# A hybrid encoder layer in split fp32: where the stationary matmul operands lie in SBUF

## The chip, the core and the metric

One core of one Trainium2 chip runs the whole program, in one launch. The metric is the device time of that launch in microseconds, as the median of three runs. Beside it stands one profiled execution, from which all rows of the profile come.

## What is computed

The reference is one inference step of one layer for 256 prompt tokens and 128 sample tokens (8 streams of 16), 384 in all, with a model width of 2048. In short:

```
u = rmsnorm(x);  P = u @ w_in          # columns: pool | z | x,B,C | dt | gates
A = causal pooling means of P.pool, mapped per group by pool_w, scaled
B = Mamba-2 scan of (conv(x,B,C), dt) + D skip, gated by silu(z), group-normed
m = sigmoid(g_A) * (A @ w_pool_proj) + sigmoid(g_B) * (B @ w_ssd_proj)
x += rmsnorm(m @ w_out)
x += rmsnorm(relu(rmsnorm(x) @ w_up)^2 @ w_down)
```

All in fp32. Outputs are x and the new pooling, convolution and scan states of both groups.

## The kernel before

**Split matmuls.** A large matrix product is made of three TensorE (PE) matmuls in the type fp32r, which takes fewer bits of a number than fp32. Each operand is split into a high part (a copy rounded to fp32r) and a low part (the rest); the product is high by high, high by low and low by high (`mm3`, L79 to L82). A matmul has a stationary operand, 128 rows by 128 columns, which is loaded first (a LDWEIGHTS row in the profile, engine PEld), and a moving operand, whose columns then stream through.

**Weights stationary.** In `proj` (L93) the weights are the stationary operand and the 384 tokens the moving one. `wfetch` (L61) loads a unit of 128 x 1024 numbers, eight tiles of 128 x 128, through the queue of SP; `wsplit` (L66) makes the high part `wh` on ScalarE (ACT, L71) and the low part `wl` on VectorE (DVE, L73); `half` (L84) issues the 24 matmuls of the unit. The pool `wpool` holds three buffers each of `w`, `wh` and `wl`. All projections by w_in (129 column tiles of two units each), w_pool_proj and w_up (two units a tile), w_ssd_proj (four) and the maps by pool_w (`pool_map`) go this way. The matmuls' names in the profile begin with `pj_`, or are `pw`.

**Activations stationary.** In `moving` (L639) it is the other way round: the weights of w_out and w_down stream as 512 columns, and tokens are the stationary operand: `mh`, `ml` for w_out (names `wo`, lines L646 to L648) and `hh`, `hl` for w_down (`wd`, the same lines).

**Stages.** First loads, the pooling columns and their maps (to 382 us about), gates and w_pool_proj (to 457 us), then for each of eight groups the conv, z and scan (to 1390 us), then w_ssd_proj (`pj_sp`, to 1656 us), w_out (to 1791 us), and the MLP in eight rounds of `pj_up` and `wd` (to 2860 us), with the last norm at the end. The scan's own matmuls (L434 to L584) are small; all but `su` (L584, stationary `bst`, moving `xst`, 256 columns, fp32r) are plain fp32, which PE takes in two records each, or transposes. Which instruction goes when on an engine is planned by the framework from the program's order and dependences; tiles get their addresses from pools, which are stacks at the left and the right end of SBUF, in steps of 32 bytes.

**Addresses.** The program's allocation gives each tile an address in the partition. Every slice of 128 columns is 512 bytes, so that a tile's place past a line of 128 bytes is also that of each of its slices. In bytes past such a line:

| operand | role | pool | place before | place after |
|---|---|---|---|---|
| wh, wl (all pj_ and pw) | stationary | wpool | 64 | 0 |
| hh, hl (wd) | stationary | phg2 | 64 | 0 |
| mh, ml (wo) | stationary | mp | 96 | 0 |
| bst (su) | stationary | phd1 | 96 | 0 |
| xs, xdw, xdt, yis, Cm, ssum, x1 (scan, transposes, norms) | stationary | phd, pha, res | 64 | 0 |
| ones (bc) | stationary | consts | 0 | 0 |
| cum, dt, dtw, nb (11 transposes, L347) | stationary | phc | 32 | 96 |
| xgh, xgl (pj_x, z, p, ga, gb, dt) | moving | xgp | 96 | 0 |
| ah, al (pj_pp) | moving | phc | 0 | 64 |
| dh, dl (pw) | moving | phc2 | 96 | 32 |
| abh, abl (pj_sp); x1h, x1l (pj_up) | moving | phe, pga | 64 | 0 |
| wh, wl (wd, wo) | moving | wpool | 64 | 0 |
| xst (su), Bk, E, hs | moving | phd | 64 | 0 |

**Lines that the change touches.** C_END and V_END (L31, L32) are the widths of the constant tiles `cst` and `vec` (L45, L46), which lie ahead of `wpool`. `small` (L142) is the first pool on the right; `tok` (L212) lies in it. At L371 to L382 the pool `phd1` gets `cstate` with its load on GpSimd's queue (POOL), the three `cbuf` with a memset each, and the two `bst` with a memset each. `mp` (L608) holds `mh` and `ml`.

Of the kernel before, what the change touches and what calls it, by code (L numbers as in the profile page):

```python
# [6 lines left out]
F32 = mybir.dt.float32  # L7
F32R = mybir.dt.float32r
# [6 lines left out]
P = 128  # L15
# [12 lines left out]
NG = 6  # L28

C_IDENT, C_ONES, C_MASK, C_CM, C_BM = 0, 128, 256, 768, 1024  # L30
C_RC, C_SCAN, C_END = 1032, 1096, 1480  # L31
V_GPRE, V_GMLP, V_PSC, V_CW, V_CB, V_NRM, V_DSK, V_DTB, V_ALOG, V_END = 0, 16, 32, 48, 240, 288, 320, 352, 353, 354  # L32


def build(ctx, tc, io):
    nc = tc.nc
    v, s, te, gp, sy = nc.vector, nc.scalar, nc.tensor, nc.gpsimd, nc.sync
# [55 lines left out]
    def proj(units, rhs, name):  # L93
        o = mmtile(f"pj_{name}")[:, :T]
        for q, src in enumerate(units):
            half(o, q, wload(src, f"{name}_{q}"), rhs)
        return o
# [44 lines left out]
    small = main.enter_context(tc.tile_pool(name="small", bufs=1, side="right"))  # L142
# [66 lines left out]
    s.copy(rstd, rms_bc(pa, acc, DM, "x"))  # L209
    pha.close()  # L210

    tok = small.tile([P, 11, NH], F32, name="tok")  # L212
    decb = small.tile([P, NH, NB], F32, name="decb")
    with tc.tile_pool(name="phc", bufs=1, reuse_waits="tile") as pc, tc.tile_pool(name="phc2", bufs=2, reuse_waits="tile") as pc2:
# [3 lines left out]
        for i in range(2):  # L218
            b = pc.tile([P, 519], F32, name=f"pbuf{i}")
# [148 lines left out]
    with tc.tile_pool(name="phd", bufs=2, reuse_waits="tile") as pd, tc.tile_pool(  # L368
        name="phd1", bufs=1, reuse_waits="tile"
    ) as pd1:  # L370
        cst_ = pd1.tile([P, 48, 9, 3], F32, name="cstate")  # L371
        gp.dma_start(cst_, io["state_conv"])
        cbuf = []
        for i in range(3):
            b = pd1.tile([P, 24, 19], F32, name=f"cbuf{i}")
            gp.memset(b[:, 0, :3], 0.0)
            cbuf.append(b)
        bst = []
        for i in range(2):
            b = pd1.tile([P, 4, 2, P], F32R, name=f"bst{i}")  # L380
            gp.memset(b.bitcast(F32), 0.0)
            bst.append(b)  # L382
        seg = lambda a: a.rearrange("p (b t) -> p b t", b=24)
        ncv = [0]

# [222 lines left out]
    mp = mpool.enter_context(tc.tile_pool(name="mp", bufs=1, side="right", reuse_waits="tile"))  # L608
    ms_ = []
    with tc.tile_pool(name="phe", bufs=1, reuse_waits="tile") as pe1, tc.tile_pool(name="phe2", bufs=3, reuse_waits="tile") as pe2:  # L610
        ab = []
        for i in range(32):
            a = pe2.tile([P, T], F32, tag="ar", name=f"ar{i}")
            sy.dma_start(a, a_scr[i])
            h = pe1.tile([P, T], F32R, name=f"abh{i}")
            l = pe1.tile([P, T], F32R, name=f"abl{i}")
            s.activation(h, a, AF.Copy)
            v.tensor_tensor(l, a, h.bitcast(F32), ALU.subtract)
            ab.append((h, l))
        for n in range(KD):  # L620
            ma = pe2.tile([P, T], F32, tag="mar", name=f"mar{n}", bufs=2)
            gb = pe2.tile([P, T], F32, tag="gbr", name=f"gbr{n}", bufs=2)
            sy.dma_start(ma, ma_scr[n])
            sy.dma_start(gb, gb_scr[n])
            ps = proj([io["w_ssd"][n, q] for q in range(4)], ab, f"sp{n}")
            v.tensor_tensor(gb, ps, gb, ALU.mult)
            v.tensor_tensor(ma, ma, gb, ALU.add)
            h = mp.tile([P, T], F32R, name=f"mh{n}")
            l = mp.tile([P, T], F32R, name=f"ml{n}")
            s.activation(h, ma, AF.Copy)  # L630
            v.tensor_tensor(l, ma, h.bitcast(F32), ALU.subtract)
            ms_.append((h, l))

    res = ctx.enter_context(tc.tile_pool(name="res", bufs=1, reuse_waits="tile"))

# [45 lines left out]
    with tc.tile_pool(name="phf", bufs=1, side="right", reuse_waits="tile") as pf, tc.tile_pool(  # L681
        name="phf2", bufs=2, side="right", reuse_waits="tile"
# [45 lines left out]
    with tc.tile_pool(name="phg", bufs=1, reuse_waits="tile") as pg, tc.tile_pool(  # L728
        name="phg2", bufs=2, reuse_waits="tile"
# [18 lines left out]
        for c8 in range(NC):  # L748
            hh = []
            for f8 in range(8):  # L750
                f = c8 * 8 + f8
# [166 lines left out]
```

## Time and profile before

| | |
|---|---|
| median of three runs | 2873.96 us (2873.9 to 2875.45) |
| span of the profiled execution, first to last instruction | 2874.5 us |
| instructions in the profile | 40193, of them 16165 matmuls and 16165 weight loads |
| PE busy | 2850.2 us, 99% |
| DVE, ACT, POOL busy | 1548.4, 1106.4, 142.2 us |
| DMA | 448.79 MB, mean 156 GB/s |

The page gives no other time of the profiled execution than its span, which is 0.5 us above the median of the runs.

In rows of the timeline the columns are start in us, duration in us, engine, line, operation, tile written and tiles read, shapes, and how many were merged into the row. A matmul's duration in the profile runs on after the next one has started, so that durations of neighbours overlap. In rows of groups (line, engine, operation) the numbers behind the bar are busy us, mean ns of one, then the engine's idle time before them and what ended it. `128*128 128x384` is a stationary operand of 128 rows by 128 columns with 384 moving columns.

### The profile page before, as it was taken

The page shows a single profiled execution, that of the slowest core. Times are in us where ns is not written, and L with a number is a line of the kernel's source. Part 1 is how long each engine was busy: PE and PEld are TensorE (multiplying, and loading weights), DVE is VectorE, ACT ScalarE, POOL GpSimd, SP SyncE. Part 2 cuts the span into 40 slices and gives each one's busy share as a digit, 9 for nine tenths or more (in the row PEclk, how much of TensorE's full clock was granted, in tenths as well). Part 3 has the DMA queues.
Part 4 walks back from the last instruction along what each step waited for, and adds up shares of the span by engine and source line. Part 5 has one row for each costly group of instructions (what it writes and reads, how often), then busy time and mean ns, then how long its engine had stood idle before and what let it go on. Part 6 is the DMA issues. An engine that isn't in the chain of part 4 may idle for free.

```text
span 2874.5 us, 40193 instructions
## 1 busy us (share of the span) xinstructions
PE 2850.2 (99%) x16165; PEld 2689.1 (94%) x16165; DVE 1548.4 (54%) x2306; ACT 1106.4 (38%) x1628; POOL 142.2 (5%) x178
## 2 busy tenths in 40 slices
PE   9999999999999999999999999999999999999998
PEld 8999999999999999999999987989898998989896
DVE  7773335668668668767543334534444444444445
ACT  5443224445445445444422233533233333333233
POOL 0000000001111011011000000000000000000001
PEclk9999999999999999999999999999999999999999
DMA  6444445456456556466644453334333333333333
GB/s 208 135 135 141 137 138 194 147 202 217 158 200 212 161 199 213 158 206 224 212 147 152 145 182 115 130 127 126 131 126 132 125 132 125 128 129 126 131 125 117
DMA packets 141914, 448.79 MB, mean 156 GB/s; under 512 B 17456, under 2 KB 41072, under 8 KB 137120
## 3 DMA queue, kind: packets, MB, share of 16 engines
q1 hardware_dynamic: 133152, 410.13, 43.7%
q0 software_dynamic: 8576, 36.11, 3.4%
q8 instruction: 126, 2.06, 0.3%
q14 instruction: 60, 0.49, 0.1%
HBM read 404.45 MB, written 41.72 MB: 155 GB/s over the span
## 4 chain that ended last, share of the span: by engine, by line
PE 97%; DVE 1%; ACT 0%; issue 0%; DVEq 0%; ACTq 0%
PE pj_up L82 6%; PE pj_up L81 6%; PE pj_up L80 6%; PE wd L647 6%; PE wd L648 6%; PE wd L646 6%; PE pj_x L82 5%; PE pj_x L80 5%; PE pj_x L81 5%; PE pj_sp L81 3%; PE pj_z L81 3%; PE pj_z L80 3%; PE pj_z L82 3%; PE pj_sp L82 3%; PE pj_sp L80 3%; PE pj_gb L80 2%
## 5 line engine op out<-in xcount | busy, mean ns | idle before, releaser
L80 PE MATMUL pj_up<-x1h,wh_up 128*128 128x384 f32 x1024 | 343.1, 335 | 0.3 <-ACT x1h L723 0.3
L81 PE MATMUL pj_up<-x1l,wh_up 128*128 128x384 f32 x1024 | 343.4, 335 | 0.0
L82 PE MATMUL pj_up<-x1h,wl_up 128*128 128x384 f32 x1024 | 342.9, 335 | 0.0
L648 PE MATMUL wd<-wh_wd,hl 128*128 128x512 f32 x768 | 298.9, 389 | 0.0
L647 PE MATMUL wd<-wl_wd,hh 128*128 128x512 f32 x768 | 298.9, 389 | 0.0
L646 PE MATMUL wd<-wh_wd,hh 128*128 128x512 f32 x768 | 298.7, 389 | 0.0
L73 DVE TENSOR_TENSOR wl_wd<-w_wd,wh_wd 128x1024 fp32r<-128x1024 f32 x128 | 156.9, 1226 | 263.0 <-ACT wh_wd L71 263.0
L71 ACT ACTIVATE wh_wd<-w_wd 128x1024 fp32r<-128x1024 f32 x128 | 135.8, 1061 | 351.1 <-PE wd L648 284.6
L73 DVE TENSOR_TENSOR wl_up<-w_up,wh_up 128x1024 fp32r<-128x1024 f32 x128 | 156.9, 1226 | 198.0 <-ACT wh_up L71 198.0
L80 PE MATMUL pj_x<-xgh,wh_x 128*128 128x384 f32 x768 | 262.8, 342 | 0.0
L71 ACT ACTIVATE wh_up<-w_up 128x1024 fp32r<-128x1024 f32 x128 | 135.7, 1062 | 326.0 <-PE pj_up L81 265.3
L82 PE MATMUL pj_x<-xgh,wl_x 128*128 128x384 f32 x768 | 259.6, 338 | 0.0
L81 PE MATMUL pj_x<-xgl,wh_x 128*128 128x384 f32 x768 | 258.2, 336 | 0.0
L80 PEld LDWEIGHTS pj_up<-x1h,wh_up 128*128 128x128 f32 x1024 | 192.5, 188 | 0.9 <-ACT x1h L723 0.6
L81 PEld LDWEIGHTS pj_up<-x1l,wh_up 128*128 128x128 f32 x1024 | 192.7, 188 | 0.4
L82 PEld LDWEIGHTS pj_up<-x1h,wl_up 128*128 128x128 f32 x1024 | 192.5, 188 | 0.1
L648 PEld LDWEIGHTS wd<-wh_wd,hl 128*128 128x128 f32 x768 | 144.1, 188 | 29.9
L647 PEld LDWEIGHTS wd<-wl_wd,hh 128*128 128x128 f32 x768 | 144.1, 188 | 29.8
L82 PE MATMUL pj_z<-xgh,wl_z 128*128 128x384 f32 x512 | 172.0, 336 | 0.0
L80 PE MATMUL pj_z<-xgh,wh_z 128*128 128x384 f32 x512 | 172.0, 336 | 0.0
L81 PE MATMUL pj_z<-xgl,wh_z 128*128 128x384 f32 x512 | 172.0, 336 | 0.0
L646 PEld LDWEIGHTS wd<-wh_wd,hh 128*128 128x128 f32 x768 | 144.2, 188 | 29.8
(280 smaller groups left out, 6228.8 us busy)
## 6 DMA issues: line engine op xcount, KB each, us to landing
w_up<-w_up SPq DMA_DIRECT2D x128, 512.0 KB, 3.5
w_wd<-w_down SPq DMA_DIRECT2D x128, 512.0 KB, 3.5
w_x<-w_in SPq DMA_DIRECT2D x96, 512.0 KB, 3.8
w_z<-w_in SPq DMA_DIRECT2D x64, 512.0 KB, 3.5
w_sp<-w_ssd SPq DMA_DIRECT2D x64, 512.0 KB, 3.5
w_ga<-w_in SPq DMA_DIRECT2D x32, 512.0 KB, 3.5
w_pp<-w_pp SPq DMA_DIRECT2D x32, 512.0 KB, 3.5
hs<-ssm SPq DMA_DIRECT2D x16, 1024.0 KB, 6.4
```

Source lines behind the costliest of these rows:

```text
L71: s.activation(h, w, AF.Copy)
L73: v.tensor_tensor(l, w, h.bitcast(F32), ALU.subtract)
L80: te.matmul(out, wh, xh, start=first, stop=False)
L81: te.matmul(out, wh, xl, start=False, stop=False)
L82: return te.matmul(out, wl, xh, start=False, stop=last)
L646: te.matmul(o[b], mh, wh[:, c], start=k == 0, stop=False)
L647: te.matmul(o[b], mh, wl[:, c], start=False, stop=False)
L648: te.matmul(o[b], ml, wh[:, c], start=False, stop=k == nk - 1)
```

## The change

Constants are widened by columns that nothing reads, two tiles of 96 bytes a partition that nothing uses are put into the pools `small` and `mp`, and the two `bst` are made ahead of `cstate` and `cbuf`. The places that result are in the last column of the table above. No other operation is added, removed or changed; the order of instructions on PE stays as it was, and on POOL the two memsets of `bst` (128x1024) go ahead of the load of `cstate` and the memsets of `cbuf`.

```
-C_RC, C_SCAN, C_END = 1032, 1096, 1480
-V_GPRE, ..., V_ALOG, V_END = 0, 16, 32, 48, 240, 288, 320, 352, 353, 354
+C_RC, C_SCAN, C_END = 1032, 1096, 1504
+V_GPRE, ..., V_ALOG, V_END = 0, 16, 32, 48, 240, 288, 320, 352, 353, 384
...
+    small.tile([P, 24], F32, name="pad_small")
     tok = small.tile([P, 11, NH], F32, name="tok")
...
+        bst = []
+        for i in range(2):
+            b = pd1.tile([P, 4, 2, P], F32R, name=f"bst{i}")
+            gp.memset(b.bitcast(F32), 0.0)
+            bst.append(b)
         cst_ = pd1.tile([P, 48, 9, 3], F32, name="cstate")
         gp.dma_start(cst_, io["state_conv"])
         cbuf = []
...
             cbuf.append(b)
-        bst = []
-        for i in range(2):
-            b = pd1.tile([P, 4, 2, P], F32R, name=f"bst{i}")
-            gp.memset(b.bitcast(F32), 0.0)
-            bst.append(b)
...
             ms_.append((h, l))
+        mp.tile([P, 24], F32, name="pad_m")
```

More of the change, by code (lines that the diff above doesn't have):

```diff
@@ L30 @@
 C_IDENT, C_ONES, C_MASK, C_CM, C_BM = 0, 128, 256, 768, 1024
-C_RC, C_SCAN, C_END = 1032, 1096, 1480
-V_GPRE, V_GMLP, V_PSC, V_CW, V_CB, V_NRM, V_DSK, V_DTB, V_ALOG, V_END = 0, 16, 32, 48, 240, 288, 320, 352, 353, 354
+C_RC, C_SCAN, C_END = 1032, 1096, 1504
+V_GPRE, V_GMLP, V_PSC, V_CW, V_CB, V_NRM, V_DSK, V_DTB, V_ALOG, V_END = 0, 16, 32, 48, 240, 288, 320, 352, 353, 384
 def build(ctx, tc, io):
```

## The prediction, made before the result was known

> **What bounds the kernel now.** I read the page first (busy shares, clock, the chain that ended last), then the busy time by stretches, then the timeline of TensorE (PE) with its start times, then the groups of weight loads.
>
> ```profile
> span 2874.5 us, 40193 instructions
> ## 1 busy us (share of the span) xinstructions
> PE 2850.2 (99%) x16165; PEld 2689.1 (94%) x16165; DVE 1548.4 (54%) x2306; ACT 1106.4 (38%) x1628; POOL 142.2 (5%) x178
> ...
> PEclk9999999999999999999999999999999999999999
> ...
> PE 97%; DVE 1%; ACT 0%; issue 0%; DVEq 0%; ACTq 0%
> ```
>
> PE is busy from end to end at the full granted clock, and 97% of the chain is PE. No engine feeds it late. So only one thing can move the time much: how far apart consecutive matmuls start. The page's "mean ns of one" doesn't tell that, because matmuls overlap; the start times do. Here are five stages; lines L80, L81, L82 (and L646, L647, L648) follow each other in turn, so from one L80 to the next are three matmuls:
>
> ```profile
> 454.76 0.34 PE L80 MATMUL pj_pp<-ah,wh_pp 128*128 128x384 f32 x1
> ...
> 455.28 0.34 PE L80 MATMUL pj_pp<-ah,wh_pp 128*128 128x384 f32 x1
> ```
> ```profile
> 860.88 0.34 PE L80 MATMUL pj_z<-xgh,wh_z 128*128 128x384 f32 x1
> ...
> 861.40 0.34 PE L80 MATMUL pj_z<-xgh,wh_z 128*128 128x384 f32 x1
> ```
> ```profile
> 2619.84 0.33 PE L81 MATMUL pj_up<-x1l,wh_up 128*128 128x384 f32 x1
> ...
> 2620.36 0.33 PE L81 MATMUL pj_up<-x1l,wh_up 128*128 128x384 f32 x1
> ```
> ```profile
> 2560.04 0.39 PE L646 MATMUL wd<-wh_wd,hh 128*128 128x512 f32 x1
> ...
> 2560.72 0.39 PE L646 MATMUL wd<-wh_wd,hh 128*128 128x512 f32 x1
> ```
> ```profile
> 1699.95 0.39 PE L646 MATMUL wo<-wh_wo,mh 128*128 128x512 f32 x1
> ...
> 1700.65 0.39 PE L646 MATMUL wo<-wh_wo,mh 128*128 128x512 f32 x1
> ```
> ```profile
> 564.09 1.12 PE L584 MATMUL su<-xst,bst 128*128 128x256 f32 x8
> 565.05 0.34 PE L81 MATMUL pj_x<-xgl,wh_x 128*128 128x384 f32 x1
> ```
>
> Three matmuls of 384 columns take 0.52 us, so 173.3 ns each; of 512 columns in wd 0.68, so 226.7; in wo 0.70, so 233.3; eight of 256 columns in su 0.96, so 120.0. From 384 to 512 columns in the wd kind is 53.4 ns for 128 columns, 0.417 ns a column. Take that off: 384 columns are 160.0, 512 are 213.3, 256 are 106.7. What is left is a **gap per matmul** that doesn't depend on its length: 13.3 ns in pj and wd, 13.3 in su, but 20.0 in wo.
>
> Now set beside it where the operands lie (the table in the section on the kernel). The moving operand makes no difference: it is at 0 past a 128 byte line in pj_pp, at 96 in pj_z, at 64 in pj_up, and all three have 13.3 ns. wo and wd run the same code with the same moving tiles; what sets them apart is the stationary operand, 96 past a line in wo and 64 in wd. So the place of the stationary operand does cost something: 6.7 ns more at 96 than at 64. Two points, 64 with 13.3 and 96 with 20.0, lie on a straight line through nothing at 0: 0.208 ns per byte past the line, or the time of 16 and of 24 columns at the rate at which weights are loaded, as these rows have it:
>
> ```profile
> L646 PEld LDWEIGHTS wd<-wh_wd,hh 128*128 128x128 f32 x768 | 144.2, 188 | 29.8
> ...
> L646 PEld LDWEIGHTS wo<-wh_wo,mh 128*128 128x128 f32 x192 | 36.0, 188 | 8.5
> L528 PEld LDWEIGHTS Y<-E,xdt 128*64 128x64 f32 x384 | 22.5, 136 | 12.6 <-issue 4.3 <-DVE yis L519 1.7 <-ACT E L492 1.7
> ...
> L511 PEld LDWEIGHTS yi<-hs,Cm 128*32 128x32 f32 x512 | 12.7, 109 | 6.1 <-issue 3.7 <-DVE hs L586 2.0 <-DMA w_gb<-w_in 0.2
> ```
>
> From 32 to 128 columns is 79 ns for 96, 0.82 ns a column; 16 columns are 13.2 ns and 24 are 19.8. The load's own recorded time, 188 in both stages, shows nothing of it.
>
> **The change part by part.** It adds and removes no instruction. The number of matmuls is the same and their order on PE as well; what moves is addresses.
>
> *Stationary operands at 64, to 0.* This is nearly everything: 129 column tiles of w_in with 48 matmuls each, 16 of w_pp with 48, 16 of pool_w with 12, 16 of w_ssd with 96, 64 of w_up with 48 make 11,760 of 384 columns, and w_down has 2,304 of 512: 14,064. No row of before has such a matmul with its stationary operand at 0, so the gap there has to be bounded. From below it is 0. From above, if the place is what makes it, the nearest row is of the fp32 matmuls, which have a load per record as well and take two passes of 128 columns, 106.7 ns:
>
> ```profile
> 681.17 0.38 PE L557 MATMUL pp<-Bk,xdw 128*128 128x128 f32 x2
> 681.39 0.39 PE L536 MATMUL Y<-cst,yis 128*128 128x128 f32 x2
> 681.61 0.39 PE L557 MATMUL pp<-Bk,xdw 128*128 128x128 f32 x2
> ```
>
> Two records start 0.22 us after the two before them, 110 ns each: 3.3 ns of gap, even at 64, where the passes leave room. I take 2 ns, between 0 and 3.3. Gain: 14,064 x 11.3 ns = 158.9 us. The other end, that 64 is as good as 0 already, is the first rival: gain 0.
>
> By the Trainium skill, TensorE: Matmul & The Clock Gate, section "Wait — 56ns, not 53.3ns?", back-to-back warm matmuls keep about 2.5 ns beyond their columns; with 2.5 in place of 2 the whole sum below would be 164 us instead of 171. The two unlike gaps of wo and wd, 20.0 and 13.3, it doesn't explain.
>
> *Those at 96, to 0.* wo has 576: 20.0 less 2 is 18.0 ns, 10.4 us. su has 128 with 13.3: 11.3 ns, 1.4 us. su doesn't fit the straight line (at 96 it should have 20); it has only 256 columns per load, so that load and matmul are about equally long, and I leave it as a warning.
>
> *The fp32 matmuls and transposes*, 1,397 of 16,165 records: at most the same 3.3 ns each, 4.6 us, taken as 0.
>
> *The two memsets of bst ahead of the load of cstate* on POOL:
>
> ```profile
> 459.05 2.06 POOL L381 MEMSET bst<- 128x1024 f32 x2
> ```
> ```profile
>   DMA cstate<-state_conv: 1.8, 1
> ```
>
> The load of cstate is issued 2.1 us later, and the copy out of it on ACT (L391), which waits 1.8 us for it now, waits about 3.9, once; the splits of w_x queue behind it. PE has up to two split units in hand then, of 24 matmuls or 4.2 us each, so I cost it at nothing; uncovered it is 2.1 us. The columns added to vec and cst are 120 and 96 bytes a partition on two loads that are made once: nothing.
>
> *What is late next.* A unit of 24 matmuls falls from 4.16 to 3.89 us. Per unit ACT and DVE need 1.06 and 1.23 us for the split, and the busy shares by stretch leave room:
>
> ```profile
> L71 ACT ACTIVATE wh_up<-w_up 128x1024 fp32r<-128x1024 f32 x128 | 135.7, 1062 | 326.0 <-PE pj_up L81 265.3
> ...
> L73 DVE TENSOR_TENSOR wl_up<-w_up,wh_up 128x1024 fp32r<-128x1024 f32 x128 | 156.9, 1226 | 198.0 <-ACT wh_up L71 198.0
> ```
> ```profile
> 0.00:210.00 210.00, 204.79 (x1148) 200.06 (x1149) 150.41 (x278) 97.92 (x171) 11.36 (x26) 1.00 0.49 160
> 457.00:1300.00 843.00, 842.64 (x5488) 809.09 (x5488) 609.67 (x1068) 401.88 (x688) 94.14 (x106) 1.00 0.57 190
> ...
> 1810.00:2860.00 1050.00, 1050.00 (x5345) 959.43 (x5345) 445.22 (x520) 349.28 (x436) 3.42 (x3) 1.00 0.39 126
> ```
>
> (after the span of the stretch: PE, PEld, DVE, ACT, POOL busy, granted clock, DMA share, GB/s). DVE is tightest, 609.67 of 843 us or 72% (150.41 of 210 us is as much, at the start); six per cent less time makes it 77%. The DMA share goes from 0.57 to 0.61. So PE stays the bound; for new waits I allow 0 to 10 us.
>
> **Sum**, against the span of the profiled execution, 2874.5: 158.9 + 10.4 + 1.4 = 170.7, so 2703.8. The median of the runs is 0.5 below that span: **2703 us**. Own range: gap 0 gives 14,192 x 13.3 + 576 x 20.0 = 200 us less, 2674; gap 3.3 gives 14,192 x 10 + 576 x 16.7 = 152 less, and 10 of new waits, 2732. With the small ends, 2670 to 2735.
>
> **The rivals.**
>
> *64 bytes is the line, and 64 is on it already.* Then 13.3 ns is simply what such a matmul costs, and only wo was off its line. For it: two points cannot tell a straight line from a step; and su, at 96, has the 13.3 of those at 64. Against it: the fp32 matmuls have 3.3, so 13.3 is not needed by every load. It gives 576 x 6.7 = 3.8 us less: 2870.
>
> By the Trainium skill, SBUF — State Buffer, note on cachelines in "Door 1: The DMA port swizzle", the line is of 16 bytes; 64 and 96 both start one, so the change would do nothing at all, 2874. The trace disagrees so far, 226.7 against 233.3 ns.
>
> *Half of it goes.* An aligned load may still hold the matmul up for a part, say 6.7 ns: 14,192 x 6.7 + 576 x 13.3 = 103 us, 2771.
>
> *Slower: the gap is the last line of the load.* A load reads 128 columns of 4 bytes. At 64 its last line holds 16 columns, at 96 it holds 24, and at 0.82 ns a column that is just 13.2 and 19.8 ns. If the matmul waits while the last line is used up, an aligned load ends with a full line of 32 columns, 26.3 ns, and the change doubles the gap: 14,192 x 13.0 + 576 x 6.3 = 188 us more, **3062**. It decides if a line that is full counts as 32 columns rather than none. The rows of before can't tell that from my forecast, since both give the same two numbers; against it, as against the forecast, is su with 13.3 at 96.
>
> *It doesn't do what it says:* by the allocation of the changed program every stationary operand is at 0, but for the eleven small transposes of L347. I give this nothing.
>
> **How the numbers follow.** Forecast 0.50 (2670 to 2735); half 0.10 (2735 to 2840); 64 is the line 0.27 (2866 to 2876); slower 0.13 (about 3062). The straight line has the better of it, because the gap is the same whole amount at three lengths and the fp32 rows show that it isn't needed; su and the lack of any row at 0 keep it at a half. The range goes from 2670 to 2876 and leaves out the slower case and a little more. About 0.2%, 5.7 us, is what a measurement of this kernel can tell from no change: faster 0.60, same 0.27 (2870 is 0.13% below), slower 0.13.
>
> **What would show it.** In the timeline of the changed kernel three matmuls of pj_up should start within 0.486 us instead of 0.52, three of wd within 0.646 instead of 0.68, and three of wo should be as near as those of wd (0.646 against 0.70). If wo falls to 0.68 and the rest stays, 64 was the line; if pj_up goes to 0.56, the last line is what counts. If the starts come nearer and the time doesn't fall by as much, PE has waits for ACT or DVE that it hasn't now, to be looked for between 457 and 1300 us. Wrong from the ground up I would be if the gap in wo came from something else than its stationary operand.

## The result and the profile after

The changed kernel takes **2888.11 us** (median of four runs, 2887.89 to 2888.59), the kernel before 2874.26 (four runs beside them). The ratio is 1.0048, with a 95% interval of 1.0034 to 1.0063: 13.9 us slower. The forecast was 2703.

The page of the changed kernel, the lines that answer to those shown of before:

```profile
span 2886.1 us, 40192 instructions
...
PE 2862.9 (99%) x16165; PEld 2702.5 (94%) x16165; DVE 1548.9 (54%) x2306; ACT 1108.4 (38%) x1628; POOL 142.4 (5%) x178
...
PEclk9999999999999999999999999999999999999999
...
PE 98%; DVE 1%; DMA 0%; ACT 0%; issue 0%; SPq 0%; DVEq 0%; ACTq 0%
```

PE is still the bound, with the same matmuls and the same clock, and busy 12.7 us longer. Where, the busy time by stages shows (start and end of the stretch in us, its length, then PE, PEld, DVE, ACT and POOL busy, granted clock, DMA share, GB/s). First the kernel before:

```profile
0.00:457.00 457.00, 451.28 (x2572) 445.85 (x2573) 245.25 (x381) 171.29 (x251) 18.92 (x40) 1.00 0.46 148
457.00:1390.00 933.00, 932.62 (x6056) 896.09 (x6055) 675.14 (x1177) 444.45 (x756) 109.16 (x127) 1.00 0.59 195
1390.00:1656.00 266.00, 266.00 (x1536) 266.00 (x1535) 105.45 (x118) 79.52 (x87) 0.54 (x1) 1.00 0.47 153
1656.00:1808.00 152.00, 147.62 (x649) 119.55 (x648) 66.31 (x95) 56.80 (x88) 3.05 (x3) 0.98 0.43 145
1808.00:2860.00 1052.00, 1052.00 (x5358) 961.39 (x5357) 446.97 (x523) 351.28 (x442) 3.42 (x3) 1.00 0.39 127
```

And the changed kernel, with the same stages:

```profile
0.00:458.00 458.00, 452.40 (x2567) 446.81 (x2568) 245.38 (x381) 171.50 (x250) 18.99 (x40) 1.00 0.46 148
458.00:1403.00 945.00, 944.95 (x6061) 908.45 (x6060) 674.67 (x1176) 444.79 (x756) 109.29 (x127) 1.00 0.59 193
1403.00:1669.00 266.00, 266.00 (x1537) 266.00 (x1536) 106.42 (x119) 80.19 (x88) 0.54 (x1) 1.00 0.50 154
1669.00:1820.00 151.00, 147.16 (x651) 119.95 (x650) 66.47 (x96) 57.16 (x90) 3.06 (x3) 0.98 0.45 146
1820.00:2872.00 1052.00, 1051.98 (x5358) 961.30 (x5356) 447.00 (x523) 351.67 (x440) 3.78 (x3) 1.00 0.40 127
```

Three stages have the time they had: w_ssd_proj, the MLP, and within a microsecond w_out. The first stage has 1 us more. The conv, z and scan stage has 12 us more, with PE busy throughout, so its matmuls themselves come slower. The timeline of PE has them (start, duration), first z, then `pj_up`, `wd` and `wo`:

```profile
870.00 0.34 PE L80 MATMUL pj_z<-xgh,wh_z 128*128 128x384 f32 x1
870.18 0.34 PE L81 MATMUL pj_z<-xgl,wh_z 128*128 128x384 f32 x1
870.35 0.34 PE L82 MATMUL pj_z<-xgh,wl_z 128*128 128x384 f32 x1
870.52 0.34 PE L80 MATMUL pj_z<-xgh,wh_z 128*128 128x384 f32 x1
870.71 0.34 PE L81 MATMUL pj_z<-xgl,wh_z 128*128 128x384 f32 x1
870.88 0.34 PE L82 MATMUL pj_z<-xgh,wl_z 128*128 128x384 f32 x1
```
```profile
2639.96 0.33 PE L82 MATMUL pj_up<-x1h,wl_up 128*128 128x384 f32 x1
...
2640.48 0.33 PE L82 MATMUL pj_up<-x1h,wl_up 128*128 128x384 f32 x1
```
```profile
2699.95 0.39 PE L650 MATMUL wd<-wh_wd,hl 128*128 128x512 f32 x1
...
2700.63 0.39 PE L650 MATMUL wd<-wh_wd,hl 128*128 128x512 f32 x1
```
```profile
1699.66 0.40 PE L649 MATMUL wo<-wl_wo,mh 128*128 128x512 f32 x1
...
1702.46 0.39 PE L649 MATMUL wo<-wl_wo,mh 128*128 128x512 f32 x1
```

Five matmuls of z take 0.88 us, 176.0 ns each, where they took 173.3. Three of `pj_up` take 0.52 and three of `wd` 0.68, to the digit as before, though their stationary operands now start a 128 byte line. The twelve of `wo` between its two rows take 2.80 us, 233.3; over the whole stage the median is 232.3. So the change gave back next to nothing where it was meant to act, and the stages with `xgh` as moving operand got slower. Summed over the trace, from each matmul's start to the next one's, their 6,192 matmuls take 1107.6 us where they took 1093.9, 13.7 us more; those of `wo` take 0.6 less. (6,192 times the 2.7 ns of this stretch would be 16.7 us; not every stretch loses as much, and the mean is 2.2 ns.) The medians of the two kernels differ by 13.9 us and the two spans by 11.6. The profiled execution of before was late already near its start: its sums of squares (`st_x`) begin at 37.0 us, those of the changed kernel at 35.3. That makes up most of what is between the two differences.

```profile
36.98 0.83 PE L116 MATMUL st_x<-cst,acc 128*128 128x2 f32 x6 [0.85 <-DVE acc L208]
```
```profile
35.31 0.73 PE L116 MATMUL st_x<-cst,acc 128*128 128x2 f32 x6
```

Theory and rivals for the runs. **R**: what counts is the *distance* between the places of the two operands, moving start less stationary start. By the allocation of the kernel before it was, in 512 bytes (the remainder when divided by 512), 416 for `xgh`, 0 for `pj_up`, `pj_sp` and `wd`, 64 for `pj_pp` and 352 for `wo`; the change made it 128 for `xgh` and 128 for `wo`, and left the others of these. **S**: the stationary operand's own place. **M**: the moving operand's own place.

### The profile page after: what moved, and what is told of

It is laid out like the page before. It is cut to its first block, busy times and chain, and to the rows that moved or that the text cites. A ratio compares the mean times of both kernels' runs of the same rounds, so it can differ in the third digit from the quotient of the medians.

```text
span 2886.1 us, 40192 instructions
## 1 busy us (share of the span) xinstructions
PE 2862.9 (99%) x16165; PEld 2702.5 (94%) x16165; DVE 1548.9 (54%) x2306; ACT 1108.4 (38%) x1628; POOL 142.4 (5%) x178
## 4 chain that ended last, share of the span: by engine, by line
PE 98%; DVE 1%; DMA 0%; ACT 0%; issue 0%; SPq 0%; DVEq 0%; ACTq 0%
PE pj_up L82 6%; PE pj_up L81 6%; PE pj_up L80 6%; PE wd L650 6%; PE wd L649 6%; PE wd L648 6%; PE pj_x L82 5%; PE pj_x L80 5%; PE pj_x L81 5%; PE pj_z L81 3%; PE pj_z L82 3%; PE pj_z L80 3%; PE pj_sp L80 3%; PE pj_sp L82 3%; PE pj_sp L81 3%; PE pj_gb L80 2%
```

## The experiments

Times and gaps of a stage below are from the trace: the mean from start to start over 24 successive matmuls, and of these means the median over the stage. The gap is that less 0.4167 ns a column (from 173.3 ns for 384 columns and 226.7 for 512). Matmuls of one stage all have the same distance, since all their tiles are multiples of 512 bytes.

**Without pad_small.** The changed kernel less one line, so that `xgh` goes back to 96 past a line.

```
-    small.tile([P, 24], F32, name="pad_small")
```

> The changed kernel without pad_small: xgh and xgl are moving operands at 96 past a 128 byte line again, all stationary operands stay at 0. In the changed kernel only the stages with xgh as moving operand got slower (176.0 ns a matmul in place of 173.3, 6192 of them, 16 us). Theory R, the place of the moving operand relative to the stationary one (moving start less stationary start, in 512 bytes) decides: that distance goes from 128 to 224, a place no run has shown; most places seen (0, 64, 416) have 173.3, so 173.3 and about 2872 us. Rival M, the moving operand's own place (128 in 512) costs: 173.3 and about 2872 us as well. Rival S, a stationary operand on its line costs in these stages whatever the moving one does: 176.0 stays, 2888 us.

2874.75 us, ratio 1.000 (0.999 to 1.001). The timeline of z:

```profile
859.98 0.34 PE L82 MATMUL pj_z<-xgh,wl_z 128*128 128x384 f32 x1
...
860.50 0.34 PE L82 MATMUL pj_z<-xgh,wl_z 128*128 128x384 f32 x1
```

0.52 us for three, 173.3. S falls: with all weights on their line z is fast or slow by where `xgh` lies. R and M stand. 13.4 us came back where 16 were expected; it is the 13.7 that the trace showed, not the 16.7 of the product.

**pad_small alone**, in the kernel before.

```
+    small.tile([P, 24], F32, name="pad_small")
     tok = small.tile([P, 11, NH], F32, name="tok")
```

> The kernel before with pad_small alone: xgh and xgl go to 128 in 512 (the start of a 128 byte line) as in the changed kernel, stationary weights stay at 64 past a line (320 in 512), distance 320. Rival M, moving operand's own place: 176.0 ns a matmul in the xgh stages as in the changed kernel, about 2874 + 16 = 2890 us. Rival S: 173.3, 2874 us. Theory R: the distance 320 is new; it gives whatever 320 gives elsewhere with the weights at 0 (the second sweep has it for pj_pp), and not the 176.0 of distance 128 unless by chance.

2874.11 us, ratio 1.000 (0.999 to 1.001).

```profile
859.80 0.34 PE L80 MATMUL pj_z<-xgh,wh_z 128*128 128x384 f32 x1
...
860.32 0.34 PE L80 MATMUL pj_z<-xgh,wh_z 128*128 128x384 f32 x1
```

0.52 us for three, 173.3, with `xgh` at exactly the place that it has in the changed kernel. So M falls too. Neither part is slow alone; the pair is.

**Two sweeps.** Unused tiles of other sizes in `small` and `mp`, and new ones ahead of `ah`, `abh`, `x1h` and `hh`, give each stage another distance, on the changed kernel. This is the edit of the first sweep; the other sweeps have other sizes.

```
-    small.tile([P, 24], F32, name="pad_small")
+    small.tile([P, 8], F32, name="pad_small")
...
+        pc.tile([P, 24], F32, name="pad_a")
...
+        pe1.tile([P, 24], F32, name="pad_b")
...
-        mp.tile([P, 24], F32, name="pad_m")
...
+    pga.tile([P, 8], F32, name="pad_u")
...
+        pg2.tile([P, 16], F32, name="pad_d", bufs=1)
```

> The changed kernel with unused tiles in several pools, so that each stage has another distance of moving to stationary operand (in 512 bytes): xgh stages 192, pj_pp 160, pj_sp 96, pj_up 32, wd 416, wo 32; stationary weights at 0. Theory R: the gap differs by distance; wo, now at 32, should not have the 18.9 ns that it has at 128, and pj_sp, pj_up, wd may leave 13.3 though nothing of their stationary weights' place has changed. Rivals M and S: stationary weights at 0 give 173.3 in pj_sp, pj_up and pj_pp whatever the moving place (S), or slow ones only where the moving operand starts a 128 byte line (M; here the xgh stages are at 64 past one, pj_sp at 96, pj_up and pj_pp at 32, so all 173.3).

2914.0 us (one run, before 2874). The matmuls of `pj_sp`, at 96, where nothing but the moving operand's place has changed:

```profile
1499.90 0.34 PE L80 MATMUL pj_sp<-abh,wh_sp 128*128 128x384 f32 x1
...
1500.96 0.34 PE L80 MATMUL pj_sp<-abh,wh_sp 128*128 128x384 f32 x1
```

Six in 1.06 us, 176.7. `wo` at 32 has 233.3, `wd` at 416 has 234.2.

> As the first sweep, with distances xgh stages 384, pj_pp 320, pj_sp 288, pj_up 256, wd 128, wo 256. Theory R: wd at 128 should show the 18.9 ns gap (232 ns a matmul) that wo has at 128 in the changed kernel, and pj_pp at 320 should have the gap of the xgh stages in the run with pad_small alone. Rival M: the xgh stages, pj_up and wd/wo (moving at 0, 128 or 256) decide by the moving place alone: wd stays at 226.7 since its moving weights stay at 0. Rival S: pj_* stay at 173.3 and wd, with its stationary operand at 384 in 512 (0 past a line), stays at 226.7.

2898.1 us (one run). `wd`, with its stationary operand on a line and its moving one where it was, at distance 128, and `wo`, at 256:

```profile
2689.63 0.40 PE L652 MATMUL wd<-wh_wd,hl 128*128 128x512 f32 x1
...
2692.43 0.39 PE L652 MATMUL wd<-wh_wd,hl 128*128 128x512 f32 x1
```
```profile
1699.80 0.39 PE L652 MATMUL wo<-wh_wo,ml 128*128 128x512 f32 x1
...
1700.48 0.39 PE L652 MATMUL wo<-wh_wo,ml 128*128 128x512 f32 x1
```

Twelve of `wd` in 2.80 us; its median over the stage is 232.3, the number of `wo` at 128 in the changed kernel. Three of `wo` in 0.68, 226.7, for the first time in these runs. `pj_pp` at 320 has 173.3, as R wanted from the run with pad_small alone.

**Weights shifted by 128 bytes.** One line more in the changed kernel; against lines of 128 bytes no weight moves, but the distances become 0 for `xgh` and 256 for `wo`.

```
+    consts.tile([P, 32], F32, name="pad_c")
```

> The changed kernel with one more unused tile of 128 bytes ahead of the weight buffers. Every stationary operand still starts a 128 byte line, and xgh still lies at 128 in 512; only the distance of moving to stationary operand goes from 128 to 0 in the xgh stages and from 128 to 256 in wo. Theory R (the distance, in 256 bytes, decides: 0 has the least gap, 128 more): xgh stages back to 173.3 ns a matmul, wo from 232.3 to 226.7; 16 us less than the changed kernel and 3.8 less than the kernel before, about 2870.5 us. Rivals M and S (own place of the moving or of the stationary operand against a 128 byte line): nothing has changed against lines of 128 bytes, 176.0 and 232.3 stay, 2888 us.

2871.19 us, ratio 0.9990 (0.9981 to 0.9999).

```profile
861.99 0.33 PE L83 MATMUL pj_z<-xgh,wl_z 128*128 128x384 f32 x1
...
862.51 0.33 PE L83 MATMUL pj_z<-xgh,wl_z 128*128 128x384 f32 x1
```
```profile
1699.83 0.39 PE L649 MATMUL wo<-wh_wo,mh 128*128 128x512 f32 x1
...
1700.51 0.39 PE L649 MATMUL wo<-wh_wo,mh 128*128 128x512 f32 x1
```

173.3 and 226.7: 16.9 us less than the changed kernel, by 128 bytes that nobody uses. In `wo` the stationary operand hasn't moved at all, and 232.3 became 226.7.

**The slow distance without any line.** The kernel before with 288 bytes in `small`: distance 128, and both operands at 64 past a 128 byte line.

```
+    small.tile([P, 72], F32, name="pad_small")
```

> The kernel before with a pad of 288 bytes in the right pool: xgh goes to 448 in 512, which is 64 past a 128 byte line, weights stay at 320, also 64 past one; the distance is 128. Theory R: 176.0 ns a matmul in the xgh stages as in the changed kernel, though no operand has been put on a line; about 2874 + 16 = 2890 us. Rivals M and S: the stationary weights haven't moved and the moving operand only goes from 96 to 64 past a line, where x1h and abh have 173.3: 173.3, 2874 us.

2888.57 us, ratio 1.0049 (1.0033 to 1.0065), the changed kernel's own time.

```profile
869.91 0.34 PE L82 MATMUL pj_z<-xgh,wl_z 128*128 128x384 f32 x1
...
870.79 0.34 PE L81 MATMUL pj_z<-xgl,wh_z 128*128 128x384 f32 x1
```

Five matmuls in 0.88 us, 176.0. With this and the run above the theory R is shown in both directions: the same places against a line go fast or slow with the distance, and the slow distance is slow at other places.

**wo alone.** The kernel before with 160 bytes in `mp`: distance 0 for `wo`.

```
+        mp.tile([P, 40], F32, name="pad_m")
```

> The kernel before with an unused tile of 160 bytes in the pool of mh and ml, nothing else: the stationary operand of wo goes from 96 to 64 past a 128 byte line, and the distance from 352 to 0. Theory R: wo falls from 233.3 to 226.7 ns a matmul, 576 x 6.7 = 3.8 us less, about 2870.5 us. Rival S in the form that a 64 byte line is what counts: the same. Rival S in the straight-line form of the prediction: also 226.7, since wd has that at 64.

2870.77 us, ratio 0.9988 (0.9979 to 0.9997), 3.6 us less than before. This and the shifted weights are the two versions with all products as exact as before that beat both kernels; their difference is within the noise. This run alone doesn't tell R from S, since the stationary place of `wo` became that of `wd` as well; the run with shifted weights does.

```profile
1699.76 0.39 PE L647 MATMUL wo<-wh_wo,mh 128*128 128x512 f32 x1
...
1700.44 0.39 PE L647 MATMUL wo<-wh_wo,mh 128*128 128x512 f32 x1
```

**Two more sweeps**, to see the period.

> A third sweep of distances on the changed kernel (in 512 bytes): xgh stages 32, pj_pp 352, pj_sp 480, pj_up 448, wo 192, wd 480. Theory R with a period of 256 bytes, from the runs so far: xgh stages 176.7 ns a matmul (as pj_up at 32), pj_pp 176.7 (352 is 96, as pj_sp at 96), pj_sp 173.3 (480 is 224, as the xgh stages at 224), pj_up 173.3 to 176.7 (448 is 192, where the xgh stages changed between both); wo at 192 and wd at 480 new for 512 columns. Rival: the period is 512, and 352, 448 and 480 need not look like 96, 192 and 224.

> A fourth sweep: xgh stages 96, pj_pp 480, pj_sp 224, pj_up 160, wo 96, wd 320. Theory R with a period of 256 bytes: xgh stages 176.7, pj_pp and pj_sp 173.3, pj_up 173.3, wo 233.3 (as at 352 in the kernel before, 352 being 96), wd at 320 (64) 226.7 if 512 columns go as 384 do there. Rival with a period of 512: 480 need not be as 224, and wo at 96 need not be as at 352.

2903.0 and 2897.1 us (one run each). All runs together, gap in ns by distance in 256 bytes:

| distance | 384 columns | 512 columns |
|---|---|---|
| 0 | 13.3 (`pj_up`, `pj_sp`, `xgh` at 0; `pj_up` at 256) | 13.3 (`wd`, `wo` at 0; `wo` at 256) |
| 32 | 13.3 or 16.7 (`pj_up` and `xgh` at 32 have both; `pj_sp` at 288 has 13.3) | 20.0 (`wo`; `wd` not tried) |
| 64 | 13.3 (`pj_pp` at 64 and 320, `xgh` at 320) | 15.5 (`wd` at 320) |
| 96 | 16.7 (`pj_sp`, `xgh` at 96; `pj_pp` at 352) | 20.0 (`wo` at 96 and 352) |
| 128 | 15.5 to 16.0 (`xgh` at 128 and 384) | 19.0 (`wo`, `wd` at 128) |
| 160 | 13.3 (`pj_pp`, `pj_up` at 160; `xgh` at 416) | 20.9 (`wd` at 416) |
| 192 | 13.3 to 16.7 (`xgh` at 192; `pj_up` at 448: 14.7) | 20.0 (`wo`) |
| 224 | 13.3 (`xgh`, `pj_sp` at 224; `pj_sp`, `pj_pp` at 480) | 20.0 (`wd` at 480) |

The period is 256 as far as tried: wherever two distances 256 apart were run on 384 columns they agree, but for those of 32 and 192, where one kernel has several paces in one stage. There a pace holds through an uninterrupted row of matmuls and changes only from one row to the next: in the first sweep, of the eight rounds of `pj_up` at 32 three keep 173.3 almost from end to end and five 176.7, at the same distance. `wd` at 320 didn't have the 226.7 that the pattern of 384 columns suggested: 512 columns have one good distance among the eight, 0, and 384 columns have four.

**wd in bf16**, both operands, their tiles at the same addresses (less exact products). Numbers are half as long, so that a slice of 128 columns takes 256 bytes; the distance stays 0 in 256.

```
+        if name.startswith("wd"):
+            h, l = h.bitcast(BF16)[:, :1024], l.bitcast(BF16)[:, :1024]
...
+                h, l = h.bitcast(BF16)[:, :T], l.bitcast(BF16)[:, :T]
```

> The kernel before with both operands of wd (high and low parts of w_down and of the hidden layer) rounded to bf16 in place of fp32r, at the same addresses; the parts keep fewer bits than fp32r, so the product is less exact. Theory G, the gap of 13.3 ns that is left at the best places belongs to the fp32r matmul with its load of 4 byte numbers: in bf16 the 512 columns should follow each other with 2 to 4 ns of gap, 216 to 217 ns a matmul in wd, 2304 x 10 = 23 us less, about 2851 us. Rival: it belongs to every pair of load and matmul: 226.7 stays, 2874 us. A gap that goes by the bytes loaded: 6.7 ns, 220 ns a matmul, 2859 us.

2848.69 us (one run, before 2874).

```profile
2549.67 0.38 PE L654 MATMUL wd<-wh_wd,hl 128*128 128x512 bf16 x1
...
2551.18 0.38 PE L652 MATMUL wd<-wh_wd,hh 128*128 128x512 bf16 x1
```
```profile
L652 PEld LDWEIGHTS <-hh 128*128 128x128 bf16 x768 | 75.1, 98 | 90.9 <-issue 1.3
```

Seven in 1.51 us, 215.7 ns; over the stage it is 215.8, 2.5 ns of gap. So the 13.3 ns don't belong to every pair of load and matmul. But the load has changed too: its recorded time is 98 ns, where the one of fp32r has 188. Whether the shorter load or the shorter numbers in the stream take the gap away, this run doesn't tell.

**The same at distance 128**, with a pad of 128 bytes ahead of `hh`.

```
+        pg2.tile([P, 32], F32, name="pad_d", bufs=1)
```

> The bf16 kernel for wd (less exact, as there) with 128 bytes of unused tile ahead of hh and hl, so that the distance of moving to stationary operand in wd is 128 in 256 instead of 0; in fp32r that distance costs 18.9 ns of gap for 512 columns instead of 13.3. Theory C, the extra comes from reads of 4 byte numbers at full rate that meet the load's reads: in bf16 it is gone, 215.2 ns a matmul as at distance 0, about 2849 us. Rival: the distance costs its 5.6 ns whatever the type: 220.8 ns, 2304 x 5.6 = 13 us more, about 2862 us.

2848.68 us (one run).

```profile
2549.69 0.38 PE L654 MATMUL wd<-wh_wd,hl 128*128 128x512 bf16 x1
...
2551.20 0.38 PE L652 MATMUL wd<-wh_wd,hh 128*128 128x512 bf16 x1
```

1.51 us again: in bf16 the distance 128 costs nothing.

## Why the prediction was wrong

*What bounds the kernel* was right, and so was the way to read it: starts, not durations. The gap of 13.3 at `pj` and `wd` and the 20.0 of `wo` in the kernel before hold over their whole stages, and the closing sentence named what would bring the forecast down: that the gap in `wo` came from something else than its stationary operand.

*The step that failed is the reading of `wo` beside `wd`*: "what sets them apart is the stationary operand, 96 past a line in wo and 64 in wd". The stationary place was indeed the one thing that differed, but with the moving tiles fixed it changes the distance along with it, and the two can't be told apart there. The moving place had been struck out because 0, 96 and 64 past a line all gave 13.3; in truth those three stages had the distances 64, 416 and 0, of the harmless ones for 384 columns all three. `wo`, at 352, was the only harmful pair among the five stages read. With `mh` on its line `wo` still has 232.3 at distance 128 and 226.7 at 256; the line has no part in it. The line through two points, 64 and 96, to nothing at 0 was then worth 159 us on paper and 0 on the chip: `pj_up` has 173.3 with its weights at 64 and at 0.

*The gap that could fall to 2 ns.* The bound of 3.3 was taken from fp32 matmuls, which PE takes in two records each; they don't stand for fp32r, whose gap doesn't fall below 13.3 at any distance tried. In bf16, with as many loads, it does. By the Trainium skill, TensorE: Matmul & The Clock Gate, section "Wait — 56ns, not 53.3ns?", 2.5 ns beyond the columns are kept by back-to-back matmuls; the bf16 run agrees with its 2.5, the fp32r runs don't.

*wo*: 10.4 us were expected, 0.6 came, since the change took it from one bad distance (352) to another (128). Distance 0 gives 3.8 by its pace, and 3.6 in the run.

*su* was to gain 1.4 us with its stationary operand from 96 to 0. Its matmuls have 121 ns in the median before and 120 after, so nothing came of it. The prediction had left it as a warning, and rightly: its place at 96, and its distance of 352, cost nothing that shows at 256 columns.

*The price that was missing*: `xgh` had been costed at nothing, as a moving operand whose place doesn't matter; pad_small and the moved weights put it at distance 128, for 13.7 us.

*The rivals.* "64 bytes is the line" had `pj` and `wd` right, but for another reason, and wanted 226.7 in `wo`, which has 232.3. "Half of it goes" wanted a gap of about 6.7 ns in `pj_up`, which still has 13.3. The last line of the load wanted 186 ns in `pj_up`, which has 173.3: refuted. That nothing at all would change (2874) holds for `pj_up` and `wd`, not for z and `wo`. The slower case had the right sign by the wrong mechanism, which is luck. None of the rivals had the two operands together.

*The memsets of bst* delay the load of cstate: in the changed kernel it is issued at 462.2 us for 458.4, and the first copy out of it on ACT starts at 469.3 for 463.9,

```profile
460.40 1.86 POOL L375 MEMSET bst<- 128x1024 f32 x2
462.19 0.54 POOL L378 DMA_DIRECT2D cstate<-state_conv  x1
```

and PE is busy for 944.95 of the 945.00 us of that stage: hidden, as forecast.

What stays open is why. In bf16 the distance 128 costs nothing and most of the gap is gone. That would fit reads of the load and of the stream that get in each other's way when 4 byte numbers stream at a column per 0.417 ns. It would as well fit a load that is over sooner, 98 ns for 188. No run here parts the two, nor tells which part of the memory they would meet in, or whether the 13.3 at the best distance is the same thing. By the Trainium skill, TensorE: Matmul & The Clock Gate, section "Step-by-step: what each phase is for", loading the next weights takes no read bandwidth from the running matmul, since each has a port of its own. In bf16 the two runs agree; in fp32r the distance between the two operands is worth up to 7.6 ns a matmul, so there the measurement decides, whatever its reason.

## What to carry to other kernels

When two stages run the same code at different pace, list every address that differs *and the differences between addresses*, and look for a stage that breaks each explanation before extending it to a point that no row has. Where fp32r matmuls bound a kernel, try the moving and the stationary operand at the same place in 256 bytes: it had the smallest gap in every stage tried here, and an absolute line of 128 bytes made no difference. A pad that seems to touch only one operand moves a pair.

## What the runs showed of the hardware that wasn't expected

- A fp32r matmul with a fresh load costs its columns plus 13.3 ns at best (173.3 for 384, 226.7 for 512), a bf16 one of `wd` plus 2.5 (215.8 for 512), with a load of 98 ns in place of 188.
- In fp32r the distance of the operands' places, in 256 bytes, adds up to 3.3 ns a matmul of 384 columns and up to 7.6 of 512; of the eight distances tried, in steps of 32 bytes, at 512 only 0 adds nothing.
- At distances 32 and 192 uninterrupted rows of matmuls of one stage go at 173.3 or at 176.7 (some at 174.7), each row keeping its pace, and a pattern of five matmuls (0.18, 0.17, 0.17, 0.19, 0.17 us) repeats at 128. So the distance alone doesn't set the delay there. That it hangs on how a row begins is a guess that no run tests.
- The recorded duration of the fp32r weight load is 187 to 190 ns in all sweeps, whatever the distance; it doesn't show what the distance costs.
